# First two token and weight blocks loaded by column halves, both token blocks on unsplit first weights, and a new opening order

## The chip, the cores and the metric

One core of one Trainium2 chip runs the kernel. The metric is the device time of one launch in microseconds (us); the runs before the change have a median of 812.9 us. Smaller is better.

## The reference, cut to what matters

The kernel computes one layer of a hybrid decoder for 512 tokens of 1024 channels. The change lies in the first step, the root-mean-square norm of the input and the projection that makes the values `v`; the rest of the layer follows it.

```python
u = _rmsnorm(h, norm1_g[l])                  # h is x: 512 x 1024, float32
proj = u @ w_in[l]                           # w_in: 1024 x 7184
a_glu, q, k, v, r, g_low, gate_a, gate_b = _split_cols(proj)
...
gk = jax.nn.log_sigmoid((g_low @ w_gate_up[l] + b_gate[l]).astype(jnp.float32)) / GATE_NORMALIZER
...                                          # conv branch, gated linear attention, merge
h = h + merged @ w_o[l]
...                                          # channel mixer, final norm
```

## The kernel before, in words

Tokens lie in four blocks of 128 (`x` tiles 0 to 3), channels in eight groups of 128. A weight tile `raw` is 128 partitions by 1024 columns of float32 (512 KB) and holds two channel groups, 512 columns each. Products need float32 precision, so a weight is split: ScalarE (ACT) rounds it to `whi`, VectorE (DVE) takes `wlo = raw - whi`, and activations are split the same way. A product is then three TensorE (PE) matmuls per channel group, high by high, high by low, low by high (`by_parts`, line 777). An unsplit float32 product (`by_raw`, line 786) needs no split but is issued by PE as two matmuls per channel group.

The opening (lines 671 to 863) computes the first 512 columns of `v` for all four token blocks and, on the way, the transposed normed tokens `u1` that every later projection reads. It stands under `manual_schedule`: PE, ACT, DVE and the DMA queue of SyncE (SP) run their instructions in the order in which the code is written. GpSimd (POOL) and everything after the opening are ordered by the scheduler.

Steps of the opening, with their lines:

- Loads (675 to 681): x0, weight 0, x1, weights 1 and 2, x2, weight 3, each whole, on SP's queue. `load_x(3)` (812) and the first four `w_glu` tiles follow as their buffers come free (three `x` buffers, four `raw` buffers). The constants `pp` and the five copies of `w_gate_up` are loaded between them (178, 874).
- `warm` (685) gives PE dummy matmuls; `turned` turns the norm's gain into one column per channel group.
- `transposed` (691) turns half of a token block, four channel groups, by four PE transposes into a PSUM bank; `with_gain` (698) multiplies by the gain on DVE into a heap tile.
- Token blocks 0 and 1 (`EARLY = 2`) are multiplied before their norm is known; the factor is applied to the result (`v_done`, 764). `squares` (716, ACT) sums a block's squares, `root` (721) takes the power on DVE and POOL. Blocks 2 and 3 are scaled first: `scale(2)` (755, ACT) must end before the transposes of x2 (836).
- Order of the products: block 0 takes weights 0 and 1 unsplit (807, 817). Block 1 takes them split (822, 823). Then both blocks take weight 2 and weight 3 (827, 837), then block 2 all four weights (851, 855) and block 3 (859).
- `split_weight(True)` splits a tile in two halves of columns (weights 0 and 1), `split_weight()` whole (weights 2 and 3).

After the opening the first `w_glu` product starts (`mm3`, line 562, from `col_tile`), and the layer goes on as one long stream of such matmuls.

## Time and profile before

| what | value |
|---|---|
| runs, median of three (lowest to highest) | 812.9 us (811.34 to 813.52) |
| profiled execution, its own time | 811.38 us |
| its span, first to last instruction | 809.7 us |
| PE busy | 802.0 us, 99% of the span |
| DVE busy | 703.2 us, 87% |
| ACT busy | 497.6 us, 61% |
| POOL busy | 191.2 us, 24% |
| mean granted TensorE clock | 0.998 |
| DMA moved | 117.94 MB, mean 146 GB/s |

The profiled execution took 1.7 us more than its span, and 1.5 us less than the median of the runs. PE's busy time is the union of its matmuls, which overlap in the pipeline; how fast PE really goes is read from the distance between the starts of two matmuls.

### The profile page before, as it was taken

How to read it: one execution, taken by the hardware profiler on the slowest of the kernel's cores; microseconds unless marked ns; L12 is line 12 of the kernel's file. 1: busy time of each engine (PE TensorE's matmuls, PEld its weight loads, DVE VectorE, ACT ScalarE, POOL GpSimd, SP SyncE). 2: the span in 40 equal slices, each digit the busy share in tenths (PEclk: the TensorE clock that was granted, in tenths of full speed). 3: DMA queues.
4: the chain of work that ended last, by engine and by line, in shares of the span. 5: the costliest groups of instructions: out<-in, count | busy, mean ns of one | idle time of the engine just before them, and what ended most of it. 6: DMA issues, size and time to landing. Idle time of an engine off the chain costs nothing.

```text
span 809.7 us, 11423 instructions
## 1 busy us (share of the span) xinstructions
PE 802.0 (99%) x4168; PEld 687.6 (85%) x4168; DVE 703.2 (87%) x1120; ACT 497.6 (61%) x763; POOL 191.2 (24%) x166
## 2 busy tenths in 40 slices
PE   9999999999999999999999999999999999999997
PEld 7888888888888899989888898898889988899886
DVE  6689999998997889786778899979976999789896
ACT  6667788677656785594445655556345663366655
POOL 2025434332204232022011101221133310522010
PEclk9999999999999999999999999999999999999999
DMA  9487758755832562432558523145732446334662
GB/s 341 146 199 183 181 168 174 166 132 143 217 84 95 168 183 81 154 106 103 158 147 204 169 81 102 62 147 157 167 119 79 144 117 166 108 105 174 165 130 105
DMA packets 46617, 117.94 MB, mean 146 GB/s; under 512 B 12552, under 2 KB 18192, under 8 KB 46560
## 3 DMA queue, kind: packets, MB, share of 16 engines
q1 hardware_dynamic: 39200, 91.24, 33.7%
q0 software_dynamic: 7200, 25.69, 18.4%
q8 instruction: 33, 0.54, 0.3%
q14 instruction: 24, 0.20, 0.1%
q10 hardware_dynamic: 160, 0.27, 0.1%
HBM read 110.76 MB, written 4.26 MB: 142 GB/s over the span
## 4 chain that ended last, share of the span: by engine, by line
PE 83%; DVE 15%; DMA 1%; issue 1%; SPq 0%; DVEq 0%
PE mm L567 19%; PE mm L566 19%; PE mm L568 19%; DVE c L928 6%; PE cv L567 4%; PE cv L566 4%; PE cv L568 4%; DVE aside L928 3%; PE ax L568 2%; PE ax L567 2%; PE ax L566 2%; PE mm L784 2%; DMA raw<-in_w_v_dram 1%; PE cv L784 1%; PE ax L1265 1%
## 5 line engine op out<-in xcount | busy, mean ns | idle before, releaser
L566 PE MATMUL mm<-uh,wlo 128*128 128x512 f32 (+1 forms) x532 | 193.7, 364 | 0.0
L567 PE MATMUL mm<-ul,whi 128*128 128x512 f32 (+1 forms) x532 | 191.6, 360 | 0.0
L568 PE MATMUL mm<-uh,whi 128*128 128x512 f32 (+1 forms) x532 | 191.3, 360 | 0.0
L441 DVE TENSOR_TENSOR wlo<-raw,whi 128x1024 fp32r<-128x1024 f32 x82 | 94.7, 1162 | 31.9 <-ACT whi L438 28.0
L406 POOL TENSOR_TENSOR raw<-raw,raw 128x512 f32<-128x512 f32 x39 | 64.7, 1658 | 236.1 <-DVE wlo L441 128.0
L566 PEld LDWEIGHTS mm<-uh,wlo 128*128 128x128 f32 x532 | 100.5, 189 | 15.5 <-DVE tmp L1434 0.3
L568 PEld LDWEIGHTS mm<-uh,whi 128*128 128x128 f32 x532 | 100.4, 189 | 15.2
L567 PEld LDWEIGHTS mm<-ul,whi 128*128 128x128 f32 x532 | 100.5, 189 | 14.8
L438 ACT CAST whi<-raw 128x1024 fp32r<-128x1024 f32 x82 | 78.8, 966 | 36.9 <-PE mm L568 16.6
L480 ACT CAST whi<-raw 128x1024 fp32r<-128x1024 f32 x80 | 83.5, 1047 | 27.3 <-PE mm L568 12.3
L489 DVE TENSOR_TENSOR wlo<-raw,whi 128x1024 fp32r<-128x1024 f32 x50 | 65.1, 1306 | 7.8 <-ACT whi L480 7.6
L438 ACT CAST whi<-kept 128x1024 fp32r<-128x1024 f32 (+1 forms) x40 | 40.2, 1009 | 31.6 <-DVE kept L382 15.6
L441 DVE TENSOR_TENSOR wlo<-kept,whi 128x1024 fp32r<-128x1024 f32 (+1 forms) x40 | 46.9, 1175 | 7.1 <-ACT whi L438 7.1
L928 DVE SCALAR_TENSOR_TENSOR c<-aside,btmp,c 128x247 f32<-128x247 f32 (+13 forms) x93 | 52.3, 567 | 0.0
L928 DVE SCALAR_TENSOR_TENSOR aside<-cv,pp,aside 128x255 f32<-128x255 f32 (+6 forms) x112 | 51.9, 463 | 0.0
L928 DVE SCALAR_TENSOR_TENSOR c<-cv,pp,c 128x247 f32<-128x247 f32 (+13 forms) x93 | 43.0, 463 | 1.3 <-POOL c L963 1.0
L482 ACT ACTIVATE wlo<-raw 128x1024 fp32r<-128x1024 f32 x28 | 29.4, 1058 | 18.7 <-PE mm L566 18.7
L1825 DVE SCALAR_TENSOR_TENSOR tmp<-mm,pp,tmp 128x511 f32<-128x511 f32 (+1 forms) x42 | 31.1, 741 | 3.5 <-ACT tmp L1822 3.4
L1431 ACT COPY tmp<-mm 128x256 f32<-128x256 f32 x38 | 14.0, 369 | 30.9 <-PE mm L568 30.3
L1825 DVE SCALAR_TENSOR_TENSOR tmp<-tmp,pp,tmp 128x511 f32<-128x511 f32 (+1 forms) x32 | 27.8, 887 | 0.4
L1587 DVE TENSOR_TENSOR hres<-hres,mm 128x512 f32<-128x512 f32 (+1 forms) x37 | 24.5, 672 | 2.2 <-PE mm L568 2.1
L567 PE MATMUL cv<-ul,whi 128*128 128x512 f32 (+1 forms) x72 | 25.6, 356 | 0.0
(517 smaller groups left out, 2080.0 us busy)
## 6 DMA issues: line engine op xcount, KB each, us to landing
raw<-in_w_up_dram SPq DMA_DIRECT2D x44, 512.0 KB, 3.4
raw<-in_w_glu_dram SPq DMA_DIRECT2D x16, 512.0 KB, 5.5
raw<-in_w_down_dram SPq DMA_DIRECT2D x16, 512.0 KB, 4.0
wlo<-in_w_glu_dram POOLq DMA_DIRECT2D x12, 512.0 KB, 7.3
kept<-in_w_down_dram POOLq DMA_DIRECT2D x9, 512.0 KB, 5.4
raw<-in_w_v_dram SPq DMA_DIRECT2D x8, 512.0 KB, 5.9
raw<-in_w_qk_dram SPq DMA_DIRECT2D x8, 512.0 KB, 6.2
raw<-in_w_gb_dram SPq DMA_DIRECT2D x8, 512.0 KB, 4.1
```

The source lines that it names most:

```text
L406: work = nc.gpsimd.tensor_tensor(out, x, y, ALU.add)
L438: nc.scalar.copy(hi, raw)
L441: two_low[:] = [nc.vector.tensor_tensor(lo, raw, hi.bitcast(F32), ALU.subtract)]
L480: nc.scalar.copy(hi, raw)
L482: pace[0] = nc.scalar.mul(lo, raw, -1.0)
L489: pace[0] = nc.vector.tensor_tensor(lo, raw, hi.bitcast(F32), ALU.subtract)
L566: nc.tensor.matmul(acc, ll, rh, start=first, stop=False, **kw)
L567: nc.tensor.matmul(acc, lh, rl, start=False, stop=False, **kw)
L568: nc.tensor.matmul(acc, lh, rh, start=False, stop=last, **kw)
L928: nc.vector.scalar_tensor_tensor(out[:, j:], x[:, : half_t - j], w, out[:, j:], ALU.mult, ALU.add)
L1587: done = nc.vector.tensor_tensor(hres[t, n][:, c], hres[t, n][:, c], acc[:, c], op)
L1825: nc.vector.scalar_tensor_tensor(z[:, s:], acc[:, : T - s], w[j], z[:, s:], ALU.mult, ALU.add)
```

## The change

All of it lies in the opening; the functions of the rest are as they were.

- x0, x1, weight 0 and weight 1 are loaded by halves of 512 columns, in this order: x0 left, weight 0 left and right, x1 left, weight 1 left and right, x0 right, weight 2 whole, x1 right, weight 3 whole, x2 whole.
- Both token blocks take weight 0 unsplit (channel groups 0 and 1). Weight 1 (groups 2 and 3) is taken split by both. The number of unsplit and of split matmuls stays the same. Splits of the activations' first half shrink to groups 2 and 3 (`RAW = 2`), 256 columns.
- Only the left half of x0 is transposed before the first product; the other halves are transposed between products.
- Weights 2 and 3 are split by halves too.
- `squares(3)` and `root(3)` come ahead of `scale(2)` and `squares(1)` instead of behind `late_acts(2)`; block 0's last product (weight 3) comes ahead of the transposes of x2 instead of behind them.
- The four `w_glu` loads come together, and `pp` and `w_gate_up` are loaded behind them; the split of `w_gate_up` (ACT and DVE) and the sums of the conv taps (DVE) come behind the opening's last work instead of amid it.

```diff
@@ loads @@
-    load_x(0)
+    load_x(0, LEFT)
+    load_by_half()
+    load_x(1, LEFT)
+    load_by_half()
+    load_x(0, RIGHT)
     load()
-    load_x(1)
-    load()
+    load_x(1, RIGHT)
     load()
     load_x(2)
-    load()
@@ split of the activations @@
+    RAW = 2
     def early_high(t, g):
-        high(eu[t, g][0], by_four(xg[t, g]))
+        ks = slice(RAW if g == 0 else 0, 4)
...
+        high(eu[t, g][0], by_four(xg[t, g])[:, ks])
@@ opening @@
-    xg[0, 0] = transposed(xs[0], 0)
-    xg[0, 1] = transposed(xs[0], 1)
-    xg[0, 0] = with_gain(xg[0, 0], 0, 2)
-    early_gain(0, 1)
+    xg[0, 0] = with_gain(transposed(xs[0], 0), 0, 2)
     highs, lows = split_weight(True)
     for half in (*highs, *lows):
         half()
-    by_raw(accs[0], 0, (0, 1))
+    by_raw(accs[0], 0, (0,))
+    tr = transposed(xs[1], 0)
+    by_raw(accs[0], 0, (1,))
+    early_high(0, 0)
+    xg[1, 0] = with_gain(tr, 0, 2)
+    by_raw(accs[1], 1, (0, 1))
+    early_low(0, 0)
...
+    squares(0)
+    tr = transposed(xs[0], 1)
+    by_parts(accs[0], 0, (2, 3))
+    xg[0, 1] = with_gain(tr, 1)
+    tr = transposed(xs[1], 1)
+    by_parts(accs[1], 1, (2, 3))
+    load_x(3)
...
     squares(2)
     root(2)
-    split_weight()
     root(0)
+    for _ in range(4):
+        load()
...
+    nc.sync.dma_start(pp, a["pp"])
+    for i in LOW_AT:
+        nc.sync.dma_start(raw_gate[i : i + RANK, :], a["gate_up"])
+    squares(3)
     scale(2)
+    root(3)
     squares(1)
     root(1)
+    by_parts(accs[0], 0, (6, 7))
     trs = [transposed(xs[2], g) for g in range(2)]
-    for t in range(EARLY):
-        by_parts(accs[t], t, (6, 7))
+    by_parts(accs[1], 1, (6, 7))
     late_acts(2, trs)
-    squares(3)
-    root(3)
```

Three places show how rows move. First SP's queue, from its fourth load on; before, with x_115 being x1, raw_117 weight 1, raw_119 weight 2, x_121 x2, raw_123 weight 3, x_179 x3 and raw_199 the first `w_glu` tile:

```order
L303 DMA raw_117<-in_w_v_dram 128x1024
L303 DMA raw_119<-in_w_v_dram 128x1024
L666 DMA x_121<-in_x_dram 128x1024
L303 DMA raw_123<-in_w_v_dram 128x1024
L178 DMA pp<-in_pp_dram 128x454
L874 DMA tmp_412<-in_gate_up_dram 16x512
L666 DMA x_179<-in_x_dram 128x1024
L303 DMA raw_199<-in_w_glu_dram 128x1024
```

Now, with x_111 being x0, x_116 x1, raw_118 weight 1, raw_122 weight 2, raw_125 weight 3, x_127 x2, x_208 x3 and raw_255 the first `w_glu` tile; x0 left, weight 0 in halves and x1 left stand ahead:

```order
L675 DMA raw_118<-in_w_v_dram 128x512 x2
L666 DMA x_111<-in_x_dram 128x512
L302 DMA raw_122<-in_w_v_dram 128x1024
L666 DMA x_116<-in_x_dram 128x512
L302 DMA raw_125<-in_w_v_dram 128x1024
L666 DMA x_127<-in_x_dram 128x1024
L666 DMA x_208<-in_x_dram 128x1024
L302 DMA raw_255<-in_w_glu_dram 128x1024
```

x2 moved behind weight 3, and x3 moved ahead of `pp` and `w_gate_up`, which now stand behind four `w_glu` tiles.

Second ACT, around the scaling of x2. Before (whi_213 and whi_242 are the high parts of weights 2 and 3, h_188 that of block 1's second half, junk the squares, of x_121 = x2, x_115 = x1 and x_179 = x3):

```order
L480 CAST whi_213<-raw_119 128x1024
L711 CAST h_188<-h_186 128x512
L718 ACTIVATE junk_236,ss_235<-x_121 128x1024
L480 CAST whi_242<-raw_123 128x1024
L756 ACTIVATE x_121<-x_121,r_47_240 128x1024
L718 ACTIVATE junk_254,ss_253<-x_115 128x1024
L711 CAST uh_100<-h_282 128x4x128
L711 CAST uh_102<-h_284 128x4x128
L718 ACTIVATE junk_291,ss_290<-x_179 128x1024
```

Now (whi_222 is the second half of weight 3's high part, h_225 the high part of block 1's second half, x_127 = x2, x_208 = x3, x_116 = x1):

```order
L722 CAST h_225<-h_220 128x512
L470 CAST whi_222<-raw_125 128x512
L729 ACTIVATE junk_245,ss_244<-x_127 128x1024
L729 ACTIVATE junk_272,ss_271<-x_208 128x1024
L768 ACTIVATE x_127<-x_127,r_46_249 128x1024
L729 ACTIVATE junk_280,ss_279<-x_116 128x1024
L722 CAST uh_100<-h_308 128x4x128
```

The squares of x2 moved behind all of weight 3, and the squares of x3 moved in between them and the scaling of x2.

Third PE, around the transposes of x2. Before (whi_242 and wlo_243 are weight 3, mm_127 and mm_128 blocks 0 and 1):

```order
L784 MATMUL mm_128<-wlo_214,h_188 128x512 x2
L695 MATMUL ax_260<-ident,x_121 128x128 x4
L695 MATMUL ax_265<-ident,x_121 128x128 x4
L784 MATMUL mm_127<-whi_242,h_154 128x512 x2
L784 MATMUL mm_127<-whi_242,h_155 128x512 x2
L784 MATMUL mm_127<-wlo_243,h_154 128x512 x2
L784 MATMUL mm_128<-whi_242,h_188 128x512 x2
```

Now (whi_222 and wlo_223 are weight 3, mm_131 and mm_132 blocks 0 and 1):

```order
L799 MATMUL mm_131<-whi_222,h_214 128x512 x2
L799 MATMUL mm_131<-whi_222,h_215 128x512 x2
L799 MATMUL mm_131<-wlo_223,h_214 128x512 x2
L706 MATMUL ax_292<-ident,x_127 128x128 x4
L706 MATMUL ax_297<-ident,x_127 128x128 x4
L799 MATMUL mm_132<-whi_222,h_225 128x512 x2
```

Block 0's six matmuls with weight 3 moved ahead of the transposes. From the first `w_glu` product on, each engine's rows stand in the same order as before, but for the split of `w_gate_up` and the tap sums, which stood amid the opening and now come behind the third `w_glu` split on ACT and DVE.

More of the change, by code (lines that the diff above doesn't have):

```diff
@@ L661, in trunk_layer, with load_x, load_by_half @@
     nc.gpsimd.memset(eps, EPS)
-    xs, rs, xg, eu = {}, {}, {}, {}
-    def load_x(t):
-        xs[t] = tp.tile([P, D], F32, tag="x", name=nm("x"), bufs=3)
-        nc.sync.dma_start(xs[t], a["x"][t * P : (t + 1) * P, :])
+    xs, rs, xg, eu, opened = {}, {}, {}, {}, []
+    def load_x(t, c=slice(0, D)):
+        if t not in xs:
+            xs[t] = tp.tile([P, D], F32, tag="x", name=nm("x"), bufs=3)
+        nc.sync.dma_start(xs[t][:, c], a["x"][t * P : (t + 1) * P, c])
+    LEFT, RIGHT = slice(0, T), slice(T, D)
+    def load_by_half():
+        name, j = order[len(raws)]
+        raw = raw_tile()
+        raws.append(raw)
+        for c in (LEFT, RIGHT):
+            nc.sync.dma_start(raw[:, c], a[name][j][:, c])
     def by_four(t):
@@ L745, in into_u1 @@
             hi, lo = in_u1(t, g)
-            low(lo, fs[g], hi)
+            opened[:] = [low(lo, fs[g], hi)]
     def normalize(t, r):
@@ L780, in by_parts @@
             for k in ks:
[L781 removed]
+                if t < EARLY:
+                    act = eu[t, k // 4][ai][:, k - RAW if k < 4 else k - 4, :]
+                else:
+                    act = acts1[k][ai][:, t * P : (t + 1) * P]
                 j = slice((k % 2) * T, (k % 2 + 1) * T)
@@ L860, in trunk_layer @@
         by_parts(acc, 3, (k, k + 1))
+    opening = list(opened)
     prefetch(LOOK)
-    v_done(3, 0, acc)
+    v_last = v_done(3, 0, acc)
     start.__exit__(None, None, None)
@@ L869, in trunk_layer @@
     bank_turns.clear()
-    raw = tmp()
-    nc.gpsimd.memset(raw, 0.0)
-    for i in LOW_AT:
-        nc.sync.dma_start(raw[i : i + RANK, :], a["gate_up"])
-    nc.scalar.copy(gate_up, raw)
+    with following([v_last]):
+        nc.scalar.copy(gate_up, raw_gate)
     rows = slice(32, 32 + RANK)
-    nc.vector.tensor_tensor(gate_up[rows], raw[rows], gate_up[rows].bitcast(F32), ALU.subtract)
+    with following(opening):
+        nc.vector.tensor_tensor(gate_up[rows], raw_gate[rows], gate_up[rows].bitcast(F32), ALU.subtract)
     ET_, OT_ = (CW + 1) // 2, CW // 2
@@ L887, in sum_taps @@
     def sum_taps():
-        first = nc.vector.tensor_tensor(taps[:, :, :OT_], cw[:, :, 0 : 2 * OT_ : 2], cw[:, :, 1::2], ALU.add)
+        with following(opening):
+            first = nc.vector.tensor_tensor(taps[:, :, :OT_], cw[:, :, 0 : 2 * OT_ : 2], cw[:, :, 1::2], ALU.add)
         tc.keep_in_program_order(first)
```

53 lines of the change are left out of this document (28 added, 25 removed).

## Prediction, made before the run

> **What bounds the kernel now.** First the page: the busy shares and the chain that ended last.
>
> ```profile
> span 809.7 us, 11423 instructions
> PE 802.0 (99%) x4168; PEld 687.6 (85%) x4168; DVE 703.2 (87%) x1120; ACT 497.6 (61%) x763; POOL 191.2 (24%) x166
> PE 83%; DVE 15%; DMA 1%; issue 1%; SPq 0%; DVEq 0%
> ```
>
> PE is busy for all but 7.7 us. A busy PE need not be PE at its peak, so the windows come next (instructions in brackets).
>
> ```profile
> 0.00:20.00 20.00, 18.38 (x83) 13.98 (x84) 12.59 (x23) 13.46 (x21) 4.64 (x19) 1.00 0.90 341
> 20.00:40.00 20.00, 20.00 (x96) 16.70 (x95) 13.29 (x21) 13.48 (x21) 1.59 (x2) 1.00 0.45 150
> 40.00:60.00 20.00, 20.00 (x90) 16.56 (x89) 16.11 (x38) 13.39 (x22) 4.40 (x5) 1.00 0.84 192
> ```
>
> From 40 us on, PE runs 90 matmuls in 20 us, one per 0.22 us, without a gap. Only the first window has idle time, and that is where the change lies. The chain in order of time says what stands at its head.
>
> ```profile
> 2.19 6.98 DMA raw<-in_w_v_dram
> 9.21 1.98 PE mm L791 x4
> 11.20 5.46 PE mm L784 x24
> 20.26 0.44 PE ax L849 x4
> 27.09 5.44 PE mm L784 x24
> ```
>
> Weight 1's load (issued at 2.19, landed at about 9.2) starts the chain, and from there it is PE work. So the launch ends earlier by what PE's waits in the opening shrink, and by no more. The waits, from the timeline of the opening (start, duration, instruction, idle time before it and what ended it):
>
> ```profile
> 4.56 0.86 PEld L695 LDWEIGHTS ax<-ident,x 128*128 128x128 f32 x8
> 4.61 1.05 PE L695 MATMUL ax<-ident,x 128*128 128x128 f32 x8
> 5.26 1.35 DVE L704 TENSOR_TENSOR h<-ax,gains 128x256 f32<-128x256 f32 x3 [0.80 <-PE ax L695]
> 5.97 1.96 PE L791 MATMUL mm<-raw,h 128*128 128x512 f32 x4 [0.31 <-DMA raw<-in_w_v_dram]
> 6.48 0.19 PEld L791 LDWEIGHTS mm<-raw,h 128*128 128x128 f32 x1 [0.24 <-issue]
> 6.91 0.19 PEld L791 LDWEIGHTS mm<-raw,h 128*128 128x128 f32 x1 [0.24 <-issue]
> 7.96 0.86 PEld L695 LDWEIGHTS ax<-ident,x 128*128 128x128 f32 x8 [0.86 <-DMA x<-in_x_dram]
> 9.21 0.30 PEld L791 LDWEIGHTS mm<-raw,h 128*128 128x128 f32 x2 [0.39 <-DMA raw<-in_w_v_dram]
> 20.46 1.18 PE L784 MATMUL cv<-whi,uh 128*128 128x512 f32 x4
> ```
>
> Prices on PE: a transpose 0.86 / 8 = 0.108 us; an unsplit matmul 6.91 - 6.48 = 0.43; a split one 5.44 / 24 = 0.227. From x0's transposes (4.61) to block 2's first product (20.46) lie 15.85 us. The work there is 24 transposes (2.6), 8 unsplit (3.4) and 36 split matmuls (8.2), and the spread of the norms (0.44): 14.6 us. So PE waits 1.2 us: 0.5 for weight 0 (5.47 to 5.97), 0.27 for x1 (7.69 to 7.96), 0.4 for weight 1 (8.82 to 9.21). The first 4.6 us, dummy matmuls, stay. **The most that any new opening order can give is 1.2 us, 0.15%.**
>
> **The change part by part.** PE's matmul count does not change; only the waits do. I follow PE.
>
> *Up to the first product.* Four transposes instead of eight end at 4.61 + 0.43 = 5.04. DVE's first gain still starts at 5.26; three instructions over 1024 columns took 1.35 us, so a 256-column piece takes about 0.34 plus some 0.1 until it is seen, 5.7. Weight 0's left half is the first 0.52 MB, as x0 was before:
>
> ```profile
> DMA to landing us min/median/max: 3.7/3.7/3.7
> ```
>
> That is x0, issued at 0.8: landed at 4.5, in time. PE starts at 5.7 instead of 5.97, but with 0.44 us less transposing behind it, so the wait grows from 0.5 to 0.66.
>
> *Weight 0 for both blocks.* Product, x1-left transposes, product, two products: 5.7 + 8 x 0.43 + 0.43 = 9.6. x1 left is needed at 6.56; it ends the first 1.05 MB, which landed at 5.86 before (below), so some 6.2 with smaller rows. Its gain on DVE (behind two halves of wlo, until about 7.2) ends near 7.7, needed at 7.9. No wait: the 0.27 and the 0.4 are gone.
>
> *x0 right* ends the first 1.84 MB. Before, 1.57 MB had landed at 7.96 and 2.10 at 9.21: 8.6, if halves move at the speed of whole rows. Their rows are 2 KB; the trace has windows of 4 KB rows (6 to 10 us) and of 1 KB rows (20.25 to 22.25), DMA share and GB/s last:
>
> ```profile
> 6.00:10.00 4.00, 3.81 (x14) 1.97 (x15) 3.70 (x7) 3.19 (x7) 0.00 (x0) 1.00 1.02 412
> 20.25:22.25 2.00, 2.00 (x13) 1.70 (x12) 1.34 (x3) 2.00 (x4) 0.55 (x1) 1.00 1.03 335
> ```
>
> 1.84 MB take 4.45 us at 412 GB/s and 5.48 at 335, so the halves cost 0 to 1.0 us; interpolating between 1 KB and 4 KB per packet gives 0.3, and 8.9. Needed on PE at 9.6. The Trainium skill (Perfetto Trace Analysis, DMA Optimizations) says that larger transfers use the memory better, from 2 KB to 4 KB too, and also that loads split in chunks let some work start sooner. By its first rule the halves would come as in rival C, by its second as in the sum; the two rows agree with the first in direction.
>
> *Weight 1, both blocks, split:* 12 x 0.227 and eight transposes, 0.87: from 9.6 to 13.2. *Weight 2:* 12 more, 15.9. *Weight 3 for block 0:* 6, 17.26. DVE feeds these from x0-right's transposes on: gain at 10.25, two halves of wlo, a low part, the next gain, each 512 columns at 0.6 (below: two in 1.29), so block 1's gain ends at 13.3 and its high part on ACT at 14.0; PE asks for it at 14.55. Margin 0.55.
>
> *The transposes of x2.* They need `scale(2)`. ACT and POOL before:
>
> ```profile
> 5.86 1.14 ACT L471 CAST whi<-raw 128x512 fp32r<-128x512 f32 x2 [3.16 <-DMA raw<-in_w_v_dram]
> 10.64 1.29 DVE L474 TENSOR_TENSOR wlo<-raw,whi 128x512 fp32r<-128x512 f32 x2
> 12.41 1.05 ACT L718 ACTIVATE junk<-x 128x1024 bf16<-128x1024 f32 x1
> 13.46 1.04 ACT L480 CAST whi<-raw 128x1024 fp32r<-128x1024 f32 x1
> 14.00 0.56 POOL L725 TENSOR_TENSOR r<-var,mhalf 128x1 f32<-128x1 f32 x1 [10.38 <-DVE var L723]
> 14.59 1.16 ACT L756 ACTIVATE x<-x,r 128x1024 f32<-128x1024 f32 x1
> 16.49 1.03 PE L695 MATMUL ax<-ident,x 128*128 128x128 f32 x8
> ```
>
> The scaling ended at 15.75, 0.7 before PE got there. Now ACT casts block 1's high part only when DVE has its gain: 13.4 to 13.9; then weight 3's second half (0.52, half of 1.14 less overlap), to 14.4; squares of x2 1.05, to 15.5; squares of x3 1.05, to 16.5; then the scaling, 1.16, to 17.7. The root of x2 (DVE, 0.56 on POOL) runs beside the squares of x3 and costs nothing. PE is there at 17.26 and **waits 0.43, a wait that was not there before.** If DVE and ACT run ahead of this, it is 0; each us that the squares of x2 or x3 come later is a us more.
>
> *From there.* Transposes 0.87, six matmuls 1.36, spread 0.4: block 2's first product at 17.7 + 2.63 = 20.36, against 20.46. One more place is tighter: only six matmuls (1.36 us) instead of twelve lie between x2's transposes and block 2. Gain and high part take 0.6 + 0.6 plus latency, and the root of x1 stands ahead of them on DVE; the high part is there at about 20.2. Margin 0.15, so I allow 0 to 0.3.
>
> *The rest.* The split of `w_gate_up` and the tap sums leave the opening for the time behind the third `w_glu` split; the 40 to 60 window hides them (DVE busy 16.11, ACT 13.39 of 20). `pp` and `w_gate_up` are issued behind weight 3's last split, at about 16 by the steps above, for first uses after 30. Queued on SP behind x3's load, which waits for x0's buffer, are only the `w_glu` tiles and these constants; they are used from 30 us on. All later rows keep their order, so the 40 to 800 us stretch carries the difference unchanged to the end.
>
> **Sum:** waits of 1.2 us become 0.66 + 0.43 and a few hundredths for starting: -0.1 us. On the profiled execution's own 811.38 us that makes 811.3. That execution was 1.5 us below the median of the runs shown, 812.9, so the same step from the median gives **812.8 us**.
>
> **The rivals.**
>
> *A, no wait for x2's scaling* (ACT runs a squares' length ahead): -0.1 - 0.43, 812.4. For it: the margins above are sums of rounded steps. Against: the row of ACT work from 13.4 on has no slack in it. 0.2.
>
> *B, slower: x3 lands late.* Its squares now stand ahead of x2's scaling, and its load waits in SP's queue for the squares of x0.
>
> ```profile
> 8.60 0.35 SPq L666 DMA_DIRECT2D x<-in_x_dram  x1
> DMA to landing us min/median/max: 6.5/6.5/6.5
> ```
>
> Before, it was issued at 8.6 and landed at 15.1. Now x0 right must land (8.9), its squares run 1.05, so it is issued at 10.0. With the same 6.5 us it lands at 16.5, a us after ACT would take it (15.5), and PE's wait grows to 1.4: +0.9 us, 813.8. The point is a landing at 15.5. Against: 0.26 MB of `pp` and `w_gate_up` no longer stand ahead of it, 0.6 us at 412 GB/s, and queued loads drain while it waits; I expect about 15. 0.2.
>
> *C, the halves move like 1 KB rows:* x0 right at 9.6 instead of 8.9, the squares of x0 and all of ACT behind them 0.7 later, PE's wait at x2 about 0.6 longer: 813.4. For it: the 335 GB/s row; against: 2 KB lies between. 0.1.
>
> *D, the clock.* The dummy matmuls at the start ran at half speed, against the transposes of the same size at 4.56:
>
> ```profile
> 1.12 2.64 PEld L687 LDWEIGHTS mm<-ones 128*128 128x128 f32 x12 [1.12 <-DVE ones L659]
> 800.00:809.70 9.70, 3.85 (x29) 3.49 (x27) 5.14 (x14) 3.57 (x11) 0.45 (x1) 0.84 0.49 191
> ```
>
> That is 0.22 us each against 0.108, and the clock falls again at the end, when PE runs dry. If it fell back in the new opening, a stretch as long as the first (1.1 to 4.4) would run at half speed: 1.65 us, 814.4. The Trainium skill (TensorE: Matmul & The Clock Gate, Part 1) has the clock go back after a window of little matmul activity, and Part 4 there does not count transposes as activity. Against: before, 4.61 to 5.97 held only transposes and waiting, and the clock stayed; now that stretch is 0.27 shorter. 0.05.
>
> **How the numbers follow.** Forecast 0.45 (812.8), A 0.2 (812.4), B 0.2 (813.8), C 0.1 (813.4), D 0.05 (814.4). All of the first four lie between -1.2 (every wait gone, 811.7) and +0.9. The median of three runs moves by itself: the runs shown lie 1.6 below to 0.6 above theirs, so I add 0.5 on each side: 811.2 to 814.3, which leaves out D's end and odd medians. A measurement of this kernel can tell about 0.3%, 2.4 us, from no change. No case but D's upper end reaches that, so within 0.3% gets 0.92; slower 0.05 (D and a late x3 with more); faster 0.03, for what I overlook, since the opening's waits are too small for it.
>
> **What would show it.** Right: no wait of PE for a DMA between 6 and 10 us; transposes of x2 waiting for ACT near 17.7; block 2's first product within 0.3 us of 20.4; the first `w_glu` matmul near 32.2. Wrong: a wait for x0 or x1 by halves, a landing of x3 after 15.5, unsplit matmuls further apart than 0.43, or any wait of PE after 40 us that was not there before.

## The result, and the profile after

The changed kernel is slower: 814.53 us against 811.48, a ratio of 1.0035 (95% interval 1.0027 to 1.0042, 12 runs each). Run again on another chip (e12 below) it took 813.66 against 811.55, 1.0029 (1.0019 to 1.0039). The forecast was 812.8, no difference that can be told, with a range that ended at 814.3. It stood on the 812.9 of three runs of before; the twelve runs here put before at 811.48. So a change of -0.1 us was forecast, and 3.05 us (2.1 on the other chip) was measured. That 813.66 lies within the range is luck: the base was 1.4 us too high.

First the page of the changed kernel and its windows, with the columns of those shown of before: PE, PEld, DVE, ACT, POOL busy, clock, DMA share, GB/s.

```profile
span 812.8 us, 11435 instructions
PE 802.3 (99%) x4168; PEld 687.5 (85%) x4168; DVE 704.6 (87%) x1124; ACT 498.2 (61%) x766; POOL 191.0 (24%) x166
PE 86%; DVE 11%; DMA 2%; issue 1%; ACT 0%; SPq 0%; DVEq 0%; ACTq 0%
```

```profile
0.00:20.00 20.00, 16.37 (x69) 11.96 (x69) 10.51 (x23) 11.52 (x20) 4.42 (x19) 1.00 0.85 309
20.00:40.00 20.00, 19.47 (x96) 16.39 (x97) 15.86 (x25) 13.78 (x21) 0.80 (x2) 1.00 0.45 139
40.00:60.00 20.00, 20.00 (x90) 16.57 (x89) 13.29 (x32) 13.62 (x19) 3.66 (x4) 1.00 0.86 207
```

PE does the same work (802.3 against 802.0 us) in a span that is 3.1 us longer. The loss is where the change is: in the first 20 us PE is busy for 16.37 us where it was 18.38, and DMA moves 309 GB/s instead of 341. From 40 us on nothing differs: the first `w_glu` matmul starts at 35.15 (before 32.37, 2.78 later), and the last matmul of the launch is 2.80 later. Another 0.3 us lies behind it and comes with the loads by halves: in the 13 profiles that have some, the span goes on for 6.38 to 6.50 us behind the start of the last matmul, in the seven with whole loads for 6.10 to 6.12. There SP waits for one semaphore after the other (line 2144, before 2110), 0.06 us each. From the landing of the last store on, two of these waits are left in the kernel before and six in the changed one.

The head of the chain of waits, in order of time:

```profile
2.19 5.68 DMA x<-in_x_dram
8.57 2.58 PE mm L806 x6
11.66 6.54 DMA x<-in_x_dram
18.39 0.86 issue
19.44 1.05 ACT x L768
20.53 1.09 PE ax L706 x8
29.87 5.44 PE mm L799 x24
```

Before, one load and then PE alone made this head. Now two loads stand in it, x1's left half (issued at 2.19, landed at 7.87) and x3 (issued at 11.66, landed at 18.2), and ACT's scaling of x2 behind the second. PE's timeline names the waits in brackets:

```profile
4.77 0.64 PE L706 MATMUL ax<-ident,x 128*128 128x128 f32 x4
5.92 1.12 PE L806 MATMUL mm<-raw,h 128*128 128x512 f32 x2 [0.52 <-DVE h L715]
7.92 0.65 PE L706 MATMUL ax<-ident,x 128*128 128x128 f32 x4 [0.87 <-DMA x<-in_x_dram]
10.99 0.60 PE L706 MATMUL ax<-ident,x 128*128 128x128 f32 x4
20.53 1.09 PE L706 MATMUL ax<-ident,x 128*128 128x128 f32 x8 [1.65 <-ACT x L768]
23.22 1.17 PE L799 MATMUL cv<-whi,uh 128*128 128x512 f32 x4
```

And ACT's rows ahead of that scaling:

```profile
14.81 0.62 ACT L722 CAST h<-h 128x512 fp32r<-128x512 f32 x1 [0.73 <-DVE h L715]
15.34 0.61 ACT L470 CAST whi<-raw 128x512 fp32r<-128x512 f32 x1
15.86 1.05 ACT L729 ACTIVATE junk<-x 128x1024 bf16<-128x1024 f32 x1
18.29 1.06 ACT L729 ACTIVATE junk<-x 128x1024 bf16<-128x1024 f32 x1 [1.28 <-DMA x<-in_x_dram]
19.34 1.13 ACT L768 ACTIVATE x<-x,r 128x1024 f32<-128x1024 f32 x1
```

The order is the one that the forecast followed: high part of block 1's second half, second half of weight 3's cast, squares of x2 (15.86), squares of x3 (18.29, after 1.28 us of waiting for its load), scaling. Each starts later than forecast, the first of these by 1.4 us, the last by 2.8.

The second profile of the same kernel (e12) differs in two things: PE's wait for x1's left half is shorter, and x3 landed at 15.06. PE, then ACT:

```profile
4.77 0.85 PE L706 MATMUL ax<-ident,x 128*128 128x128 f32 x4
6.14 1.13 PE L806 MATMUL mm<-raw,h 128*128 128x512 f32 x2 [0.52 <-DVE h L715]
7.49 0.66 PE L706 MATMUL ax<-ident,x 128*128 128x128 f32 x4 [0.23 <-DMA x<-in_x_dram]
10.57 0.60 PE L706 MATMUL ax<-ident,x 128*128 128x128 f32 x4
18.80 1.09 PE L706 MATMUL ax<-ident,x 128*128 128x128 f32 x8 [0.33 <-ACT x L768]
```

```profile
15.38 1.05 ACT L729 ACTIVATE junk<-x 128x1024 bf16<-128x1024 f32 x1
16.56 1.06 ACT L729 ACTIVATE junk<-x 128x1024 bf16<-128x1024 f32 x1
17.61 1.13 ACT L768 ACTIVATE x<-x,r 128x1024 f32<-128x1024 f32 x1
```

Its first `w_glu` matmul starts at 33.41, 1.04 behind before, and its span is 811.1. Of the 1.7 us between the two, 0.4 was there at x0's right half (10.99 and 10.57), and 1.3 came with x3. So one late load can set two executions of this kernel more than a microsecond apart, and a single profile has to be read with that in mind. With the 1.7 us that lay around the span of before, the two make 814.5 and 812.8: the first chip's median, and the fastest run on the second (812.83).

### The profile page after: what moved, and what is told of

Same layout as the page of the kernel before. It is cut to its first block, busy times and chain, and to the rows that moved or that the text cites. A ratio compares the mean times of both kernels' runs of the same rounds, so it can differ in the third digit from the quotient of the medians.

```text
span 812.8 us, 11435 instructions
## 1 busy us (share of the span) xinstructions
PE 802.3 (99%) x4168; PEld 687.5 (85%) x4168; DVE 704.6 (87%) x1124; ACT 498.2 (61%) x766; POOL 191.0 (24%) x166
## 4 chain that ended last, share of the span: by engine, by line
PE 86%; DVE 11%; DMA 2%; issue 1%; ACT 0%; SPq 0%; DVEq 0%; ACTq 0%
PE mm L566 20%; PE mm L565 20%; PE mm L567 20%; DVE c L962 5%; PE cv L566 4%; PE cv L565 4%; PE cv L567 4%; DVE aside L962 3%; PE ax L566 2%; PE ax L565 2%; PE ax L567 2%; DMA x<-in_x_dram 2%; PE mm L799 1%; PE ax L1299 1%; PE cv L799 1%
## 5 line engine op out<-in xcount | busy, mean ns | idle before, releaser
L437 ACT CAST whi<-raw 128x1024 fp32r<-128x1024 f32 x82 | 78.9, 966 | 36.8 <-PE mm L567 16.6
L479 ACT CAST whi<-raw 128x1024 fp32r<-128x1024 f32 x78 | 81.5, 1048 | 27.6 <-PE mm L567 12.3
```

The lines of the kernel that those rows point to most:

```text
L437: nc.scalar.copy(hi, raw)
L479: nc.scalar.copy(hi, raw)
```

## The experiments

Each run stands beside the kernel before on the same chip. "w_glu" is the start of the first `w_glu` matmul in the profiled execution (before: 32.37).

| run | median, us | before there | ratio (95% interval) | w_glu |
|---|---|---|---|---|
| changed kernel | 814.53 | 811.48 | 1.0035 (1.0027 to 1.0042) | 35.15 |
| e12 changed kernel again | 813.66 | 811.55 | 1.0029 (1.0019 to 1.0039) | 33.41 |
| e1 whole loads | 813.48 | 811.52 | 1.0022 (1.0013 to 1.0031) | 33.87 |
| e2 old order, column halves | 812.77 | 811.52 | 1.0013 (1.0004 to 1.0022) | 33.33 |
| e8 old order, even and odd rows | 814.87 | 811.66 | 1.0045 (1.0028 to 1.0063) | 34.46 |
| e5 old order, upper and lower rows | 815.29 | 811.52 | 1.0047 (1.003 to 1.0064) | 35.58 |
| e4 weights on ACT's queue | 816.68 | 811.66 | 1.0062 (1.0045 to 1.0078) | 35.52 |
| e11 halves on two queues | 816.70 | 811.55 | 1.0061 (1.0047 to 1.0075) | 35.60 |
| e15 the same, with dummies | 814.58 | 811.55 | 1.0037 (1.0025 to 1.005) | 34.68 |
| e16 whole weights, x by halves | 813.29 | 811.59 | 1.0024 (1.0016 to 1.0033) | 33.02 |
| e18 the same, with dummies | 812.88 | 811.57 | 1.0015 (1.0006 to 1.0024) | 33.24 |
| e17 e16 with squares moved | 813.50 | 811.59 | 1.0027 (1.0016 to 1.0038) | 33.29 |
| e3 squares of x3 back | 814.01 | 811.52 | 1.0032 (1.0019 to 1.0045) | 34.38 |
| e7 old order, squares of x3 early | 812.36 | 811.66 | 1.0008 (0.9999 to 1.0018) | 33.73 |
| e6 whole loads, x3 early | 812.95 | 811.66 | 1.0016 (1.0007 to 1.0026) | 33.48 |
| e9 e6 with squares of x2 early | 812.28 | 811.55 | 1.0008 (0.9999 to 1.0018) | 32.61 |
| e14 e9 with dummies | 812.22 | 811.55 | 1.0010 (1.0001 to 1.0019) | 32.87 |
| e10 changed kernel with dummies | 813.64 | 811.55 | 1.0026 (1.0015 to 1.0036) | 34.07 |
| e13 before with dummies | 812.04 | 811.55 | 1.0005 (0.9996 to 1.0014) | 33.04 |

Two theories stood at the start: H, the halves land late; X, the new order (x3's load and squares) costs.

**e1, the changed kernel with whole loads.**

```diff
-    load_x(0, LEFT)
-    load_by_half()
-    load_x(1, LEFT)
-    load_by_half()
-    load_x(0, RIGHT)
+    load_x(0)
+    load()
+    load_x(1)
+    load()
     load()
-    load_x(1, RIGHT)
     load()
     load_x(2)
```

> The changed kernel with its first blocks loaded whole again (x0, weight 0, x1, weights 1, 2, 3, x2), the new order of the work kept. Theory H (the halves are the cost: they land late): the first product is again set by weight 0 near 5.97, x1 lands at 7.9 and x0 is complete at 4.5, and the loss goes: 811.5 to 812.0 us. Theory X (the cost is the new order: the load of x3 waits for the squares of x0, and its squares stand ahead of the scaling of x2): x1 whole lands at 7.9, just when x1 left does in the changed kernel, the squares of x0 still stand behind weight 1 on ACT (about 10.5), x3 is issued near 11.6 and the transposes of x2 still start at 19.5 to 20.5: 814 to 814.5 us.

In between, 1.0022: with whole loads 1.96 us of the loss are left, so the late halves aren't the whole of it. DMA ran at 388 GB/s from 4 to 8 us (changed kernel 255), and still PE waited 0.8 us for x1: whole, x1 is the third load and lands at 7.94, after 1.57 MB, no sooner than its half did. The order was built on an x1 half that comes early, and pays when it doesn't.

**e2, the kernel before with x0, weight 0, x1 and weight 1 by column halves,** old order.

```diff
-    load_x(0)
-    load()
-    load_x(1)
-    load()
+    load_x(0, LEFT)
+    load_x(0, RIGHT)
+    load_by_half()
+    load_x(1, LEFT)
+    load_x(1, RIGHT)
+    load_by_half()
```

> The kernel before with x0, x1, weight 0 and weight 1 loaded by column halves, left then right, in the old order of tiles. Theory H: weight 0 is complete when the changed kernel's fourth half landed, 7.9 instead of 5.86, x1 at 9.7 instead of 7.96, weight 1 at about 11 instead of 9.2; block 2's first product comes 1.7 us later: 813.0 to 813.4 us. Theory X: halves cost at most 0.3 us, 811.3 to 811.8 us.

Halves alone cost 1.0013 (1.0004 to 1.0022), 1.25 us: more than X had and a little less than H. The window from 4 to 8 us, first of e2, then of the kernel before:

```profile
4.00:8.00 4.00, 3.46 (x14) 2.55 (x13) 1.86 (x5) 0.62 (x1) 0.00 (x0) 1.00 0.74 226
```

```profile
4.00:8.00 4.00, 3.65 (x17) 2.12 (x16) 2.91 (x7) 2.14 (x4) 0.00 (x0) 1.00 0.99 387
```

226 instead of 387 GB/s, at a share of 0.74. The engines stood idle for a quarter of the time. The median packet was as quick as elsewhere (84 ns for 2 KB; 159 for the 4 KB of before), but some took far longer, so that the mean was 105 ns. The next four microseconds of e2 look different:

```profile
8.00:12.00 4.00, 4.00 (x16) 2.12 (x16) 3.55 (x7) 3.45 (x7) 0.00 (x0) 1.00 1.00 387
```

Here the halves still in the queue landed at 8.13, 8.83, 9.45 and 10.09, some 0.65 us apart, which is the pace of whole loads (1.23 to 1.25 us for each 512 KB in the kernel before, from 9 us on). The changed kernel's two profiles show the same (9.06, 9.65, 10.30; and 7.45, 8.09, 8.74, 9.39). The first two halves of e2 were not slow either (3.66 and 4.34). So halves are late from 4 to 8 us of the launch, and not by themselves.

**e8 and e5, the kernel before with the same four tiles by halves of rows:** 4 KB rows, 64 partitions a load, even and odd ones (e8) or upper and lower ones (e5).

```diff
+    LEFT, RIGHT = slice(0, P, 2), slice(1, P, 2)             # e8
+    LEFT, RIGHT = slice(0, P // 2), slice(P // 2, P)         # e5
+            nc.sync.dma_start(raw[c, :], a[name][j][c, :])
```

> The kernel before, old order, with x0, weight 0, x1 and weight 1 each loaded as two transfers of 64 partitions, the even and the odd ones, with whole rows of 4 KB: 256 KB per load as with the halves of columns, twice their row. Theory L (a cost for each load on each engine makes the column halves slow): as with column halves in the old order, 812.8 us, first w_glu matmul near 33.3, windows of 200 to 300 GB/s. Theory W (the 2 KB rows do): 811.5 us, near 400 GB/s from 4 us on. Theory P (64 partitions are reached at half the rate, as with the upper and lower 64): a load lands each 1.13 us, windows of 210 to 260 GB/s at a full share of the engines, 815.3 us.

> As the kernel before with halves, in the old order, but the halves are 64 partitions with whole rows of 4 KB instead of 128 partitions with rows of 2 KB: the same number of loads and the same bytes in each. If a load costs the queue a fixed time whatever its size, x0 to weight 1 land as late as with column halves: 813.0 to 813.4 us. If it is the 2 KB rows (twice as many rows for the same bytes), they land as whole tiles do: 811.3 to 811.8 us.

The same window, e8 and then e5:

```profile
4.00:8.00 4.00, 3.01 (x13) 2.52 (x13) 1.60 (x4) 0.43 (x1) 0.00 (x0) 1.00 0.84 231
```

```profile
4.00:8.00 4.00, 2.92 (x12) 2.24 (x12) 1.19 (x4) 0.05 (x1) 0.00 (x0) 1.00 1.04 230
```

With twice the row, e8 moves no more than the column halves: the row's length isn't it. Theory W falls, and with it the interpolation by row length in the forecast. In e8 it is more the slow packets (a mean of 235 ns, a median of 159) and less the idle time. From 8 to 12 us e8 comes back to 382 GB/s. e5 does not: it has 230 GB/s there too, with engines full and a median packet of 292 ns instead of 159, so its slowness is another one and says nothing on the size of a load. (The times of e8 and e5 hold more than their loads: ACT's table load, 1.28 us, ran at 7.57 and 7.95 there and at 1.42 in e2. So the 814.87 of e8 is no proof of theory P with its 815.3; P wanted the engines full, and e8's share was 0.84.)

**e4 and e11, two queues.** e4 issues the halves of weights 0 and 1 on ACT's queue; e11 alternates the halves between SP's and ACT's, in the order of the change.

```diff
-            nc.sync.dma_start(raw[:, c], a[name][j][:, c])
+            nc.scalar.dma_start(raw[:, c], a[name][j][:, c])     # e4
-    load_by_half()
-    load_x(1, LEFT)
-    load_by_half()
+    load_by_half(nc.scalar, nc.sync)                             # e11
+    load_x(1, LEFT, nc.scalar)
+    load_by_half(nc.sync, nc.scalar)
```

> The changed kernel with the four halves of weights 0 and 1 issued on ACT's DMA queue instead of SP's; x0 and x1 halves and the rest stay on SP. Theory Q (one queue can't feed the DMA engines with loads of 256 KB, and two can): between 4 and 8 us the engines' share is near 1.0 at some 400 GB/s instead of 0.6 to 0.9 at 220 to 290; x0 right lands near 8.9 (10.3 in the changed kernel), x3 near 16.5 (18.2), the first w_glu matmul comes near 33.2 (35.15), 812.6 us. Rival M (it lies in the transfers, whatever queue they come from: a cost per load on each DMA engine, or the 2 KB rows): the windows stay at 220 to 290 GB/s, x0 right near 10.3, the first w_glu matmul near 35, 814.5 us.

> The changed kernel with its halves issued by turns on SP's and ACT's queue, in the order of the change: x0 left on SP, weight 0 left on ACT and right on SP, x1 left on ACT, weight 1 left on SP and right on ACT, x0 right and the rest on SP. Theory Q (a queue loses a fixed time on each load, and two queues overlap it): the loads land by 7 to 9 us as fast as whole ones, x1 left near 6.7 (7.87), x0 right near 9 (10.3), x3 is issued near 10.4 and lands near 17, first w_glu matmul near 33.7, 813.1 us. Rival M (the loss is on the engines or in memory, whatever the queue): 220 to 290 GB/s between 4 and 8 us as changed, x0 right near 10.3, first w_glu matmul near 35, 814.5 us.

Both are the slowest of the set, so a second queue is no remedy; with the same dummies added, two queues (e15, 814.58) were no faster than one (e10, 813.64) either. In e11 DMA moved 287 GB/s from 4 to 8 us, x1's left half landed at 8.88, x0's right at 9.37. In e4 it was 307 GB/s, and weight 1's right half landed last, at 11.68. Another cause came to light in both. PE in e11, then in e15, which is e11 with dummy matmuls in PE's waits:

```profile
4.77 1.06 PE L706 MATMUL ax<-ident,x 128*128 128x128 f32 x4
6.35 2.08 PE L806 MATMUL mm<-raw,h 128*128 128x512 f32 x2 [0.52 <-DVE h L715]
```

```profile
4.48 0.60 PE L706 MATMUL ax<-ident,x 128*128 128x128 f32 x4
4.92 0.83 PE L698 MATMUL mm<-ones 128*128 128x128 f32 x6
6.09 1.10 PE L806 MATMUL mm<-raw,h 128*128 128x512 f32 x2 [0.34 <-DMA raw<-in_w_v_dram]
```

The same two products take 2.08 us in e11 and 1.10 in e15. In e11, e4 and e5 PE's matmuls stayed at the dummies' half speed until about 10 us; in the other 17 profiles (both profiles of the changed kernel among them) they doubled between 4.4 and 7.6. That opened a third theory, D: waits of PE in the opening delay its full speed in some executions.

**e15, e11 with dummies; e10, the changed kernel with dummies; e13, before with dummies; e12, the changed kernel again.**

```diff
     xg[0, 0] = with_gain(transposed(xs[0], 0), 0, 2)
+    warm(3)                                             # e10, e15
...
+    warm(4)                                             # e10, e15
     tr = transposed(xs[1], 0)
...
     xg[0, 1] = transposed(xs[0], 1)
+    warm(2)                                             # e13
...
+    warm(2)                                             # e13
     by_raw(accs[0], 0, (2, 3))
```

> The changed kernel with three dummy matmuls on PE behind x0-left's transposes and four ahead of x1-left's, in PE's waits of 0.57 and 0.93 us; loads and all else as changed. Theory D (part of the loss is that PE's matmuls, which take twice as long at the start, come to full speed later in some executions because PE waits in the opening): the median falls by 0.3 to 0.8 us, to 813.7 to 814.2, and the highest runs (815.9) go. Rival (the waits leave PE's speed alone, all of the loss is in the landings and what follows them): the same 814.5 within 0.2 us, since the dummies lie in waits; the first w_glu matmul near 35.1.

> The changed kernel itself, beside the next three on the same chip. Both theories: 814.5 us. Its second profile tells how far landings move from one execution to the next: theory L (the late x3 of the first profile, 6.5 us from issue to landing, is the rule) has x3 land near 18.2 again and x2's transposes near 20.5; theory S (one DMA engine was late by chance) has it land near 16 and x2's transposes near 19.4, with the first w_glu matmul near 34.

> The version with the halves by turns on two queues, with dummy matmuls in PE's waits as in the changed kernel with dummies (three and four). Theory D: PE is at full speed by 6.5 us, the first unsplit products take 0.43 us each instead of 0.85, and the 816.7 of the two queues falls to 813.5 to 814.5. Rival (something else in the two-queue version is slow): 816 or more.

> The kernel before with two dummy matmuls behind x0's transposes and two ahead of block 0's product with weight 1, in PE's waits of 0.5 and 0.4 us. Theory D (waits in the opening let PE come to full speed late in some executions): before's waits are short and few, so little is to be had: 811.2 to 811.5 us against 811.55. Rival: the dummies stand in the way of the first product, 811.7 to 812.0.

e10 seemed to bear D out, 0.9 us below the first result; e12 took that back, since the changed kernel without dummies came to the same 813.66. For e11 the times speak for D: 816.7 fell to 814.6, and though the two intervals just overlap, each of e15's five runs is faster than each of e11's four. The profiles don't show that the dummies did it by the speed. In e15 the transposes at 4.48 ran at full speed already, ahead of the first added dummy (4.92), and e11's profiled run, with its late doubling, was the fastest of its four. Before gains nothing from dummies (1.0005). So the dummies helped e11; that they did so as D has it is likely and not shown, and for the changed kernel nothing is shown.

**e16, the changed kernel with weights 0 and 1 whole and only the tokens by halves; e18, the same with three dummies ahead of the first product.**

```diff
     load_x(0, LEFT)
-    load_by_half()
+    load()
     load_x(1, LEFT)
-    load_by_half()
+    load()
     load_x(0, RIGHT)
...
+    warm(3)                                             # e18
```

> The changed kernel with weights 0 and 1 loaded whole; x0 and x1 still by halves, the order of loads and all else as changed. Theory L (each load of 256 KB costs, so fewer of them land sooner): x1 left, the third load and 1.05 MB, lands at 6.2 to 6.6 (7.45 to 7.87 in the changed kernel), PE doesn't wait for it, x0 right lands near 8.6, the first w_glu matmul comes at 32.4 to 32.9 and the median is 812.2 to 812.8 us (813.7 to 814.5 as changed). Rival T (the slow stretch from 4 to 8 us belongs to the order, x1's half behind weight 0, or to the start of the launch, not to the cut): x1 left after 7.2, 813.5 us or more.

> The version with whole weights and x by halves, with three dummy matmuls on PE behind x0-left's transposes, in its wait of 0.5 us ahead of the first product. Theory D (in the upper group of runs PE's matmuls come to full speed only near 10 us, because PE waits there): the group at 814.5 to 815.0 is gone, the median falls from 813.3 to 812.6 to 813.0 us. Rival (the groups come from landing times): two groups again, with the median at 813.2 to 813.6.

PE in e16:

```profile
6.22 1.13 PE L806 MATMUL mm<-raw,h 128*128 128x512 f32 x2 [0.52 <-DVE h L715]
7.18 0.60 PE L706 MATMUL ax<-ident,x 128*128 128x128 f32 x4
18.44 1.09 PE L706 MATMUL ax<-ident,x 128*128 128x128 f32 x8 [0.35 <-ACT x L768]
```

x1's left half landed at 6.15 (6.23 in e17, 6.05 in e18), and PE's wait for it is gone: there is no bracket at 7.18. The same 1.05 MB had landed at 7.45 to 7.88 when weight 0 was halved too. Fewer early halves land sooner, as theory L had it. Over the whole set the windows from 4 to 8 us are ordered in the same way: 340 to 416 GB/s in the seven profiles with whole loads, 290 to 319 with the tokens halved, 226 to 294 with tokens and weights halved by columns on one queue. Rival T falls as far as it blames the order, which e16 kept. Its other half, the start of the launch, is part of the answer, since halves after 8 us are not slow. The median, 813.29, came out above what L had for it (812.2 to 812.8), because the runs fell in two groups, 812.5 to 813.4 and 814.5 to 815.0. With dummies one run of eleven lay above 813.3 (814.14). That points to D, but the two intervals overlap, so it isn't shown.

**e3 and e7, the squares of x3.** e3 puts them back behind x2's late work in the changed kernel; e7 moves them ahead in the kernel before.

```diff
-    squares(3)
     scale(2)
-    root(3)
...
     late_acts(2, trs)
+    squares(3)
+    root(3)
```

> The changed kernel with the squares and the root of x3 put back behind the late activations of block 2, so that the scaling of x2 waits for the squares of x2 alone. Theory X: the scaling starts at about 17.9 instead of 19.3, the transposes of x2 at 19.0 instead of 20.5, and the time falls by 1.2 to 1.5 us against the changed kernel, to 813.1. Theory H: the scaling is late because everything ahead of it on ACT is late, so x3's place gives 0 to 0.3 us.

And e7:

```diff
     root(0)
+    squares(3)
     scale(2)
+    root(3)
...
     late_acts(2, trs)
-    squares(3)
-    root(3)
```

> The kernel before with only the squares and root of x3 moved ahead of x2's scaling, as the change has them; loads and all else as before. Theory X (the squares of x3 ahead of the scaling are a loss even when x3 lands early): x3 lands at 15.1, its squares run 15.2 to 16.2, the scaling ends at 17.3, x2's transposes start at 17.4 instead of 16.49, nothing is given back: +0.9 us, first w_glu matmul near 33.3, 812.4 us. Rival (the squares only trade places on ACT, and what x3 no longer needs later is given back at x3's transposes): 0 to 0.2 us, 811.5 to 811.7.

PE in e7:

```profile
17.78 1.09 PE L695 MATMUL ax<-ident,x 128*128 128x128 f32 x8 [0.83 <-ACT x L756]
```

A wait of 0.83 us for the scaling, where there was none, as X had it; the median moved by 0.7, within the uncertainty. e3's x2 was transposed at 18.93, with a wait of 0.19, but then x3's transposes waited 0.62 for its own scaling: of the 1.6 us by which block 2 came earlier than in the first profile 0.8 were left at the first `w_glu` matmul, and the time can't be told from the changed kernel's.

**e6, whole loads, x0's right half transposed before the first product and its squares behind it, squares of x3 back; e9, e6 with the squares of x2 moved to where ACT waited for DVE; e14, e9 with dummies; e17, e16 with e3's and e9's moves.**

```diff
     xg[0, 0] = with_gain(transposed(xs[0], 0), 0, 2)
+    tr = transposed(xs[0], 1)                           # e6, e9, e14
...
+    squares(0)
+    xg[0, 1] = with_gain(tr, 1)
+    load_x(3)
+    trs = [transposed(xs[1], g) for g in range(2)]
...
+    squares(2)                                          # e9, e14, e17
+    root(2)
     highs, lows = split_weight(True)
-    highs[0]()
     early_high(1, 1)
+    highs[0]()
     highs[1]()
```

> The changed kernel with whole loads in the order x0, weight 0, x1, weights 1, 2, 3, x2, with x0's right half transposed before the first product and its squares right behind (so that x3 can be issued near 8.4 instead of 11.7), both halves of x1 transposed together, and the squares of x3 back behind x2's late work. Both token blocks still take weight 0 unsplit and weight 1 split, in halves, as in the changed kernel. Theory S (the loss is the halves' landings, the late issue of x3 and its squares ahead of x2's scaling, and nothing else): PE waits in the opening sum to 0.6 us, x2's transposes near 17.5 without a wait for ACT, block 2's first product near 20.2, the first w_glu matmul near 32.1, 811.2 us (before 811.5). Rival R (the shared unsplit products, the split of weight 1 by both blocks and the shorter cover behind x2's transposes cost by themselves): the first w_glu matmul at 33 or later, 812.4 us or more.

> The version with whole loads and x3 early, with the squares and the root of x2 moved ahead of the high part of block 1's second half and of weight 3's casts on ACT, where ACT waited from 12.6 to 13.8 for DVE. Theory C (what that version still lost is the place of x2's scaling in ACT's line, 0.6 us, and 0.2 to 0.5 of landing times): x2's transposes start near 17.5 with no wait for ACT, block 2's first product near 20.2, first w_glu matmul at 32.1 to 32.6, 811.5 to 812.0 us against 811.6 of before. Rival R (the shared unsplit products and the splits by halves cost by themselves): the wait at x2 goes, another takes its place on DVE's line, first w_glu matmul at 33 or later, 812.6 us or more.

> The version with whole loads, x3 early and x2's squares early, with two dummy matmuls in the wait ahead of the first product. Its PE waits are shorter than those of before, so theory D and its rival both say 812.0 to 812.3 us (812.28 without them); under 811.5 would be a version that beats both kernels.

> The version with whole weights and x by halves, with the squares and root of x3 back behind x2's late work and the squares and root of x2 ahead of the high part of block 1's second half and of weight 3's casts. Theory L with what the other runs showed of ACT's line: x2's transposes wait for nothing, near 17.2, the first w_glu matmul at 31.9 to 32.5, 811.0 to 811.8 us against 811.55 of before. Rival T: x1 left after 7.2, the first w_glu matmul at 32.8 or later, 812.3 us or more.

e6 missed its forecast by 1.8 us: PE lost 0.3 us ahead of x2's transposes (18.02) and waited 0.62 for x3's scaling (24.34), because ACT stood from 12.6 to 13.8 waiting for DVE's gain, with the squares of x2 and all that follows queued behind. e9 moved them: x2's transposes came at 17.61, x3's wait fell to 0.24, and the first `w_glu` matmul came at 32.61, at the edge of what theory C had; the median, 812.28, lies above its 811.5 to 812.0. e9's PE waits over the whole launch:

```profile
PE mm L696 <- DVE ones L658: 1.1, 1, 1.1
PE cv L565 <- DVE hres L1617: 0.3, 1, 0.3
PE ax L646 <- DVE ul L651: 0.3, 1, 0.3
PE ax L704 <- ACT x L766: 0.2, 1, 0.2
```

In the opening the view has one wait of 0.2 us, apart from the launch's first; two waits of 0.3 stand near 456 and 473 us, and e14's profile has neither. So with whole loads, x3 issued early and x2's scaling in time, both token blocks on unsplit weight 0 come out close to before: 1.0008 (0.9999 to 1.0018) in e9, which can't be told from it, and 1.0010 (1.0001 to 1.0019) in e14, which just can. e17 did not get there: x2 landed at 13.4, ACT waited for it 1.57 us ahead of block 1's high part, and PE for that part.

No version was faster than the kernel before.

## Why the prediction was wrong, step by step

The forecast's own times, beside the two profiles of the changed kernel:

| step | forecast | first profile | second |
|---|---|---|---|
| first product | 5.7 | 5.92 | 6.14 |
| x1 left landed | 6.2 | 7.87 | 7.45 |
| x0 right landed | 8.9 | 10.30 | 9.39 |
| transposes of x0 right | 9.6 | 10.99 | 10.57 |
| squares of x2 | 14.4 | 15.86 | 15.38 |
| x3 landed | about 15 | 18.2 | 15.06 |
| transposes of x2 | 17.7 | 20.53 | 18.80 |
| block 2's first product | 20.36 | 23.22 | 21.49 |
| first `w_glu` matmul | 32.2 | 35.15 | 33.41 |

**The step that failed is "some 6.2 with smaller rows", and with it "No wait: the 0.27 and the 0.4 are gone".** It took the halves at the speed of whole loads, and priced a slower one (0.3 us) by the length of the row. What the runs showed is that from 4 to 8 us of the launch loads of 256 KB land late whatever their rows: on one queue 1.05 MB landed at 7.45 to 8.13 in four loads, at 6.05 to 6.23 in three with weight 0 whole, and at 5.74 to 6.05 as two whole loads. PE's wait for x1 was not removed but grew, from 0.27 to 0.87 (0.23 in the second profile). Whole loads in the new order don't mend the step, since x1 is then the third load and lands at 7.94 (e1, still 1.96 us slower than before). Only with weight 0 whole and the tokens halved did x1's left half come when the forecast had it; 1.3 to 1.9 us of loss were left even then (e18, e16, e17), of which the halves' 0.4 us at the kernel's end is one part.

**The shift then ran through unhindered.** Up to the transposes of x0's right half the first profile is 1.4 us behind the forecast (0.2 at the first product, 1.0 for x1, the rest at changes between transposes and products), the second 1.0 (0.4, 0.4 and the rest). Every later step of DVE and ACT hangs on those transposes, and each is late by the same 1.0 to 1.5 us. The forecast's margins of 0.15 to 0.55 us lay between steps that all moved together, so they held and hid nothing.

**x3, rival B.** Its mechanism came true in the first profile, with a PE wait of 1.65 where it had 1.4. Its 6.5 us from issue to landing came out at 6.54 (3.83 in the second profile). x3 was issued at 11.66, not at 10.0, since its buffer waits for the squares and the transposes of x0's right half, both late. Fourteen of its sixteen engine shares were in by 15.40, near the forecast; the last one came at 18.20. ACT waited 1.28 us, which makes up the rest of the 2.8 us at x2's transposes (1.4 + 1.3). In the second profile x3 was in time and this term is nil. The change put ACT's whole line behind one load, and how late the slowest share of that load is differs from one execution to the next.

**The first product,** 5.7 forecast, came at 5.92 and 6.14, because the last dummies and the transposes of x0 still ran partly at half speed: the transposes start at 4.77 instead of 4.61, and four of them take 0.64 and 0.85 us, against 0.60 later in the same profiles. The row of before that gave the price was taken after the speed had doubled, at about 4.5; in most other profiles it doubles later.

**What held.** The order of the instructions, the prices of matmuls, transposes, squares and casts, the wait for x2's scaling (0.33 in the second profile, forecast 0.43), the 0.87 + 1.36 + 0.4 from there to block 2 (20.53 + 2.69, and 18.80 + 2.69, forecast 2.63), and no new wait of PE after 40 us. Rival A falls, since the wait for x2's scaling came. Rival C had halves that land late, though by the length of their rows, which isn't the cause, and its 9.6 for x0's right half lies between the 9.39 and 10.30 measured; it missed that x1's left half, on which PE waits first, is late by more. Rival D's half speed was seen, but in e4, e5 and e11, not in a profile of the changed kernel. The bound of 1.2 us on any gain was not tested, since no version tried beat before.

**The chances** failed with the range: its lower cases were worked out to a tenth of a microsecond, while one unmeasured quantity, the speed of 256 KB loads from 4 to 8 us, bore on every step. C's price for it came from two windows that differed in row length and not in the size or place of the load. And the upper end was the worst single rival, B, with 0.5 us of spread: in the first profile late halves and a late x3 came together, 1.4 and 1.3 us. That the base was 1.4 us too high hid part of the miss.

What stays open: why loads of 256 KB leave the engines idle and some packets slow from 4 to 8 us of the launch, and not later; and whether PE's late full speed is part of the changed kernel's median. Halves and order could not be added up from single undoings: e1 and e3 each gave back less than e9, which undid both.

## What to carry to other kernels

Before splitting a load so that its first part comes sooner, find a row of the trace with loads of that size at that place in the launch: here halving weight 0 and the tokens made the first 1.05 MB land 1.4 to 2.4 us later than two whole loads, though halves behind 8 us were not slow; halving the tokens alone kept the early half. When a new order puts a load's consumer ahead of a step that the critical engine needs, price the slowest execution of that load, not the median one, and take a second profile before trusting a difference of a microsecond. Where steps are chained, a margin between two of them is no cover for a delay of both.

## What the runs showed of the hardware that was not expected

- From 4 to 8 us of the launch, loads of 512 KB over 128 partitions kept the DMA engines at a share of 0.99 and 387 GB/s in the kernel before; loads of 256 KB gave 226 (columns, e2) and 231 (even and odd partitions, e8). From 8 to 12 us these two had 387 and 382. Upper and lower partitions (e5) gave 230 GB/s in both windows, with the engines full and a median packet of 292 ns. Two queues gave 277 to 307 from 4 to 8 us (e15, e11, e4). The Trainium skill (DMA: Bandwidth & Descriptors, Anatomy of one DMA) gives each DMA a fixed cost of about 2 us, most of it the receipt of the last write; it measured that on another path of issue. A fixed cost per load agrees in direction with the early windows of e2, e8 and e16, but the halves that landed some 0.65 us apart behind 8 us show none; what the cost before that consists of, no run here shows.
- A load has landed when the slowest of its sixteen shares has, and that share can trail: x3's by 2.8 us in the first profile, weight 0's right half by 1.6 (eleven shares in by 5.46, the last at 7.05).
- The moment at which PE's matmuls double their speed moved between executions, from 4.4 to at most 7.6 us in 17 profiles and to about 10 in three, while the granted clock of the windows read 1.00 throughout. The Trainium skill (TensorE: Matmul & The Clock Gate, Part 1) has a free-running window of 3.4 us decide it, which would move it by half a microsecond from run to run; the 17 are spread over more than that, and the three at 10 are further off still. In all three PE waited 0.5 us or more around x0's transposes, but so it did in profiles that were not late. Dummies in those waits took 2.1 us off e11's median; that the doubling came sooner through them no profile shows, since in e15 it came ahead of the first of them.
